# Seven products in place of eight for twelve block pairs of a float32 projection, and weight staging moved one stage later

## The chip, the cores and the metric

One NeuronCore of one Trainium2 chip runs the kernel. The metric is the device time of one execution in microseconds (us). Five engines work side by side, each through its own instructions in order: TensorE (PE), VectorE (DVE), ScalarE (ACT), GpSimd (POOL), and SyncE (SP), whose one queue issues all the DMAs that matter here.

## What is computed

The kernel is one inference step of a two-layer decoder trunk over 1032 token columns: 1024 of a prompt and 8 of single-token samples. The part that the change touches is the end of layer 0, cut from the reference:

```
q, k, v, g, a_low, hb, gate_b, gate_c, z_b = split(h @ w_in)   # h = rmsnorm(x), 1024 wide
o = gla(q, k, v, ...) ; o = rmsnorm(o) * silu(g)
y = causal_dwconv(gate_c * hb, buf, w_sconv)                   # 3 taps, "short convolution"
y = gate_b * y * silu(z_b)
x = x + concatenate([o, y]) @ w_out                            # output projection, 2048 -> 1024
```

Layer 1 follows: a pointwise projection of 1024 to 3072 with a gate, a depthwise convolution 31 wide, a LayerNorm, a second gate, a projection of 1024 to 1024, and a final norm.

## The kernel before, in words

**Products.** Activations lie with channels on partitions and tokens along the free axis. The 1032 columns are cut into three chunks `CH` of 384, 384 and 264. A weight block is 1024 x 128, stored as 128 x 1024 (eight slices of 128 x 128, one for each k). Weights and activations are each split into a rounded high part and the rest, and a product is the sum of three passes in the order `"hxw"`: high by high, high weight by low activation, low weight by high activation. So one block and one chunk make a `unit` (L232) of 8 x 3 = 24 matmuls into one PSUM bank, and a block costs three units.

**Weights.** `plan` lists the blocks in the order of use. `load_ahead` issues the load into one of two `raw` buffers (L199). `split_ahead` lets ACT write the high part `wh` (L219) and POOL the rest `wl` (L220), into pools of three buffers each. `W(key, ahead)` hands out a block and splits `ahead` blocks further. Layer 1's 32 blocks are split earlier by `stage_weights` (L182 to L190): load `pw`, ACT `ph` (L186), POOL `pl` (L187), two stores of 0.5 MB to DRAM (`wh_d`, `wl_d`), so that layer 1 only loads the two parts.

**Order.** ACT's instructions run as the program is written. The tile scheduler orders the other engines by its own estimates. Side work (staging, the state of the long convolution) is a generator that `tick()` moves on after each unit, once a count has been reached: `start(job, at)`. A ring of 25 tiles (`T`) serves nearly all the intermediate tiles, and four PSUM banks the units.

**Short convolution** (L620 to L658). For each of eight i it takes four blocks: gate_c into `cs` (L626), hb into `ch` (L630), three taps on ACT and DVE (L633 to L640), z_b into `zs` with silu (L647, L649), then POOL multiplies `y` by the norm `rs` (L650) and by `zs` (L651), and the gate_b units end it (L655), with the high and low part of `y` written chunk by chunk into `Bm` (L656, L657). Staging starts in it at tick 20 (`STAGE_AT`), and `conv_state` at tick 52.

**Output projection** (L663 to L720). The o tiles are read back from DRAM (`ol`), ACT and DVE write their high and low parts into `O` (L669, L670; `O` takes the buffers of the normed input `A`). Each of eight f runs three units of 48 matmuls, the eight `Bm` terms and the eight `O` terms together:

```
        wy = W("o", f, 1)
        wo = W("o", f, 0, ahead=1)
        for c, (lo, n) in enumerate(CH):
            terms = [(wy[0][:, k * P:(k + 1) * P], ..., Bm[k][1][:, s]) for k in range(KT)] + a_terms(wo, O, c)
```

## Time and profile before

| | |
|---|---|
| median of 3 runs | 1323.96 us (1322.83 to 1327.75) |
| the profiled execution, its own time | 1324.79 us |
| its span, first to last instruction | 1323.0 us |
| GLA with its projections | 0 to about 381 us of the span |
| short convolution | about 381 to 741 us |
| output projection | 741 to about 923 us |
| layer 1 and the final norm | 923 to 1323 us |
| PE, DVE, POOL, ACT busy | 97%, 54%, 49%, 37% |
| DMA | 171.55 MB, mean 130 GB/s |

The stage bounds are read from the lines that the engines run. The profiled execution lies 0.83 us above the median, and 1.79 us of its time lie outside the span. A window's columns are its length, then busy time and instruction count of each engine, the granted TensorE clock as a share of full speed, the mean busy share of the 16 DMA engines, and the rate.

### The profile page before, as it was taken

To read this page: it belongs to the slowest core of one execution; us is meant where nothing else is said; L and a number is where in the kernel's file an instruction comes from. 1 tells how busy PE (TensorE), PEld (TensorE's weight loads), DVE (VectorE), ACT (ScalarE), POOL (GpSimd) and SP (SyncE) were. 2 spreads that over 40 slices of the span, in tenths; PEclk is the share of its full clock that TensorE was granted. 3 is DMA by queue.
4 is the path that set the end of the run, shared out by engine and by line. 5 is a ranking of instruction groups with operands and counts; after the bars stand their busy time and mean duration, and the time that the engine had idled before them with its cause. 6 is when DMAs were issued, how large, how long until landed. Compare 5 with 4: busy or idle time off the path is not lost.

```text
span 1323.0 us, 20294 instructions
## 1 busy us (share of the span) xinstructions
PE 1286.8 (97%) x8333; PEld 1263.3 (95%) x8333; DVE 711.5 (54%) x1081; ACT 492.4 (37%) x753; POOL 651.4 (49%) x400
## 2 busy tenths in 40 slices
PE   7999999998999999999999999999999999999995
PEld 7999999997999999999999999999899999998995
DVE  6444547648546223434424411114769899979726
ACT  7422515233323132222322411113373737437513
POOL 1354525426254357667675221212288898947202
PEclk9999999999999999999999999999899999999997
DMA  7013033221231176777674731213222223223413
GB/s 254 33 64 132 32 97 118 96 96 68 93 138 70 59 255 241 256 267 264 245 271 164 258 117 49 85 45 111 72 94 90 88 91 100 96 96 117 172 64 128
DMA packets 59068, 171.55 MB, mean 130 GB/s; under 512 B 7248, under 2 KB 21296, under 8 KB 58976
## 3 DMA queue, kind: packets, MB, share of 16 engines
q1 hardware_dynamic: 58704, 169.99, 36.6%
q8 instruction: 65, 1.06, 0.3%
q10 hardware_dynamic: 272, 0.27, 0.1%
q14 instruction: 27, 0.22, 0.1%
HBM read 118.06 MB, written 52.18 MB: 129 GB/s over the span
## 4 chain that ended last, share of the span: by engine, by line
PE 79%; DVE 7%; DMA 7%; POOL 2%; ACT 2%; issue 1%; SPq 0%; DVEq 0%; POOLq 0%; ACTq 0%
PE mm L238 66%; PE mm L314 8%; DMA pw<-in_dram 6%; DVE s L541 1%; ACT ph L186 1%; PE g L532 1%; DVE cv L904 1%; DVE x L684 1%; PE g L475 1%; PE g L535 1%; PE g L514 1%; PE g L476 1%; POOL wl L220 1%; DMA s<-in_dram 1%; DVE Y L998 1%
## 5 line engine op out<-in xcount | busy, mean ns | idle before, releaser
L238 PE MATMUL mm<-A,wh 128*128 128x384 f32 (+1 forms) x2304 | 388.1, 319 | 1.4 <-DVE zs L647 1.4
L238 PEld LDWEIGHTS mm<-A,wh 128*128 128x128 f32 x2304 | 364.9, 188 | 2.9 <-DVE zs L647 2.0
L220 POOL TENSOR_TENSOR wl<-wr,wh 128x1024 fp32r<-128x1024 f32 x70 | 176.1, 2519 | 242.3 <-ACT wh L219 125.3
L238 PE MATMUL mm<-A,wl 128*128 128x384 f32 (+1 forms) x1152 | 204.0, 318 | 0.0
L238 PE MATMUL mm<-X,wh 128*128 128x384 f32 (+1 forms) x1152 | 199.3, 323 | 3.4 <-ACT X L686 2.4
L238 PEld LDWEIGHTS mm<-X,wh 128*128 128x128 f32 x1152 | 184.2, 189 | 8.3 <-ACT X L686 5.1
L238 PEld LDWEIGHTS mm<-A,wl 128*128 128x128 f32 x1152 | 184.7, 188 | 0.0
L187 POOL TENSOR_TENSOR pl<-pw,ph 128x1024 fp32r<-128x1024 f32 x32 | 78.8, 2463 | 78.0 <-ACT ph L186 64.7
L785 POOL TENSOR_TENSOR pa<-pa,pr 128x1024 f32<-128x1024 f32 x45 | 110.6, 2458 | 13.0 <-ACT pr L783 10.8
L314 PE MATMUL mm<-wh,A 128*128 128x256 f32 (+3 forms) x576 | 108.8, 288 | 6.9 <-ACT A L259 6.9
L219 ACT ACTIVATE wh<-wr 128x1024 fp32r<-128x1024 f32 (+1 forms) x72 | 75.3, 1052 | 82.1 <-PE mm L238 65.3
L238 PE MATMUL mm<-X,wl 128*128 128x384 f32 (+1 forms) x576 | 103.9, 321 | 0.0
L771 DVE SCALAR_TENSOR_TENSOR g<-u,late,g 128x512 f32<-128x512 f32 x150 | 102.2, 748 | 1.3 <-ACT g L768 1.3
L314 PEld LDWEIGHTS mm<-wh,A 128*128 128x128 f32 (+1 forms) x576 | 87.5, 182 | 8.8 <-ACT A L259 6.9
L238 PEld LDWEIGHTS mm<-X,wl 128*128 128x128 f32 x576 | 94.0, 191 | 0.1
L314 PE MATMUL mm<-wl,A 128*128 128x256 f32 (+3 forms) x288 | 82.8, 288 | 0.0
L704 DVE TENSOR_TENSOR x<-mm,x 128x384 f32<-128x384 f32 (+1 forms) x24 | 12.4, 515 | 126.0 <-PE mm L238 126.0
L186 ACT ACTIVATE ph<-pw 128x1024 fp32r<-128x1024 f32 x32 | 33.9, 1058 | 118.9 <-DMA pw<-in_dram 114.3
L238 PE MATMUL mm<-M,wh 128*128 128x384 f32 (+1 forms) x384 | 66.5, 324 | 2.8 <-ACT M L920 1.7
L238 PE MATMUL mm<-O,wh 128*128 128x384 f32 (+1 forms) x384 | 68.2, 319 | 0.0
L238 PEld LDWEIGHTS mm<-M,wh 128*128 128x128 f32 x384 | 61.9, 191 | 4.2 <-ACT M L920 2.0
L238 PEld LDWEIGHTS mm<-O,wh 128*128 128x128 f32 x384 | 61.5, 188 | 0.1
(225 smaller groups left out, 1906.5 us busy)
## 6 DMA issues: line engine op xcount, KB each, us to landing
wr<-in_dram SPq DMA_DIRECT2D x70, 512.0 KB, 3.6
pw<-in_dram SPq DMA_DIRECT2D x32, 512.0 KB, 5.5
wh_d<-ph SPq DMA_DIRECT2D x32, 512.0 KB, 3.8
wl_d<-pl SPq DMA_DIRECT2D x32, 512.0 KB, 4.5
wh<-wh_d SPq DMA_DIRECT2D x32, 512.0 KB, 3.5
wl<-wl_d SPq DMA_DIRECT2D x32, 512.0 KB, 4.4
bc<-dec_d SPq DMA_DIRECT2D x12, 512.0 KB, 5.7
o_d<-o SPq DMA_DIRECT2D x8, 516.0 KB, 2.9
```

Of the source, the lines that this page charges most:

```text
L186: act.activation(h, r, AF.Copy)
L187: pool.tensor_tensor(out=l, in0=r, in1=h.bitcast(F32), op=ALU.subtract)
L219: act.activation(h[:, :n], raw[:, :n], AF.Copy)
L220: e.tensor_tensor(out=l[:, :n], in0=raw[:, :n], in1=h[:, :n].bitcast(F32), op=ALU.subtract)
L238: pe.matmul(out, wl if p == "w" else wh, xl if p == "x" else xh, start=(i == 0), stop=(i == len(seq) - 1))
L314: pe.matmul(ps[:m, :width], x, y[:, ks], start=(i == 0), stop=(i == 23))
L475: pe.matmul(ps[:, j * P:(j + 1) * P], ke[:, lo:lo + P], qe[:, lo:lo + P], start=True, stop=True)
L476: pe.matmul(ps[0:64, j * P + 64:(j + 1) * P], kd[:, lo:lo + 64], qe[:, lo + 64:lo + P], start=True, stop=True)
L514: pe.matmul(ps[:, j * DV:(j + 1) * DV], kt[:, p_, :], V[Q][:, p_ % 4, :], start=True, stop=True)
L532: pe.matmul(ps[:, j * P:(j + 1) * P], V[Q][:, j, hs], scT[:, Q, j * P:(j + 1) * P], start=True, stop=(p_ == 0))
L771: dve.scalar_tensor_tensor(out=acc[r], in0=u[:, 1 - r, lo + j:hi + j], scalar=df(r, j), in1=acc[r], op0=ALU.mult, op1=ALU.add)
L785: pool.tensor_tensor(out=ac, in0=ac, in1=pr, op=ALU.add)
```

## The change

**Seven products.** The 32 blocks of the short convolution are taken in 16 pairs q (gate_c with hb, then gate_b with z_b). For q = 3 to 14 the first two chunks of a pair, which are 2 blocks x 2 halves of k x 2 chunks = 8 products of 12 matmuls, are done by Strassen's scheme in Winograd's form (`pair_products`): seven `product`s of 12 matmuls, with sums and differences of weights (`pair_sums`, four DVE additions of 128 x 512, whose results `s0` and `s1` are split like a block) and of activations (`build_t`, from tick 10, into twelve tiles `tq` that stay in the ring). The third chunk keeps its unit. ACT copies the first product to `u2`, DVE adds up the others, and `done` multiplies the 768 columns by the norm afterwards. `first_pair` overwrites half of `A[1]` with one of the differences, and `put_back` restores it before q = 15. The first three pairs and the last one run units as before.

**Gated y.** z_b and gate_b now come in one pair, so `y` is finished by POOL (times `gt`, times `zs`) at the end of each i, stored to DRAM (`y_d`), and for i < 7 read back at the end (`all_parts`) to be split into `Bm`. The last one is split from `y` itself after `finish()`, ahead of `O` in the program.

**Output projection.** Each f except the last first runs the three `O` units of 24 matmuls, then the three `Bm` units into the same banks (`into=sums[c]`).

**Staging.** `conv_state` and `stage_weights` start in the output projection, and only 11 blocks go through the latter. Sixteen go through the weight pool as entries `("stage", n)` between the o blocks, with two stores each. The last five of the final projection are not staged: they are loaded and split where they are used.

```diff
-OSQ_WAIT, STATE_AT = 4, 52
+OSQ_WAIT, STATE_AT = 4, 1
...
-STAGE_AT = 20
+STAGE_AT, BUILD_AT = 4, 10
+STRASSEN = range(3, 15)
+RING_STAGED, OWN_STAGED = 11, 16
...
+    for q in range(2 * KT):
+        m0, m1 = blocks_of(q)
+        if q in STRASSEN:
+            for part, src in (("w0", flat(wa[m0])), ("s0", flat(wa[m1])), ("s1", None), ("w1", None)):
+                plan.append(((part, q), src, KT * P, pool, wp))
+        else:
+            plan_a(m0)
+            plan_a(m1)
...
+    owned = list(range(RING_STAGED, RING_STAGED + OWN_STAGED))
     for f in range(KT):
-        for j in (1, 0):
+        for j in (0, 1):
             plan_w(("o", f, j), woa[f, j], pool)
-
-    staged = []
-
-    def plan_d(key, src):
-        plan.append((key, len(staged), KT * P, None, None))
-        staged.append(src)
-
-    for i in range(KT):
-        for j in (8, 0):
-            plan_d(("c", j + i), wic[j + i])
-    for i in range(KT):
-        plan_d(("c", 16 + i), wic[16 + i])
-    for f in range(KT):
-        plan_d(("f", f), woc[f])
-    raws, parts, used = [], [], [0]
+            if owned:
+                plan.append((("stage", owned[0]), flat(staged[owned.pop(0)]), KT * P, pool, wp))
...
+    for i, key in enumerate(keys):
+        if i < RING_STAGED + OWN_STAGED:
+            plan.append((key, i, KT * P, None, None))
+        else:
+            plan_w(key, staged[i], pool)
...
-        for i, src in enumerate(staged):
+        for i, src in enumerate(staged[:RING_STAGED]):
...
+            key, src, n, e, where = plan[len(parts)]
             raw = raws[len(parts)]
+            if key[0] == "s0":
+                pair_sums(key[1])
+            if key[0] in ("s0", "s1"):
+                raw = sums_of[key[1]][key[0] == "s1"]
+            elif key[0] == "w1":
+                raw = raws[len(parts) - 2]
...
+            if key[0] == "stage":
+                sp.dma_start(out=wh_d[key[1]], in_=h[:, :n].bitcast(F32))
+                sp.dma_start(out=wl_d[key[1]], in_=l[:, :n].bitcast(F32))
+
+    def pair_sums(q):
+        if q not in sums_of:
+            e0 = next(i for i, p in enumerate(plan) if p[0] == ("w0", q))
+            load_ahead(e0 + 2)
+            a, b = raws[e0], raws[e0 + 1]
+            s0, s1 = T([P, KT * P], s="s0"), T([P, KT * P], s="s1")
+            lo, hi = slice(0, 512), slice(512, 1024)
+            dve.tensor_tensor(out=s0[:, lo], in0=b[:, lo], in1=b[:, hi], op=ALU.add)
+            dve.tensor_tensor(out=s0[:, hi], in0=s0[:, lo], in1=a[:, lo], op=ALU.subtract)
+            dve.tensor_tensor(out=s1[:, lo], in0=a[:, lo], in1=b[:, lo], op=ALU.subtract)
+            dve.tensor_tensor(out=s1[:, hi], in0=a[:, hi], in1=s0[:, hi], op=ALU.subtract)
+            sums_of[q] = s0, s1
...
+    def unit(c, terms, mid=None, into=None, part=(True, True)):
+        out = mm_t()[:, :CH[c][1]] if into is None else into
         seq = [(t, p) for p in ORDER for t in terms] if ORDER[0] != "k" else [(t, p) for t in terms for p in ORDER[1:]]
         for i, ((wh, wl, xh, xl), p) in enumerate(seq):
-            pe.matmul(out, wl if p == "w" else wh, xl if p == "x" else xh, start=(i == 0), stop=(i == len(seq) - 1))
+            pe.matmul(out, wl if p == "w" else wh, xl if p == "x" else xh, start=(into is None and i == 0),
+                      stop=(part[1] and i == len(seq) - 1))
...
-    start(conv_state(), STATE_AT)
-    start(stage_weights(), STAGE_AT)
...
+        for k in range(4):
+            a, b = T([P, 2 * n], s="xa"), T([P, 2 * n], s="xb")
+            for t, kk in ((a, k), (b, k + 4)):
+                sp.dma_start(out=t, in_=xT[:, kk, 0:2 * n])
+                act.activation(t, t, AF.Copy, scale=pcol("g0", kk))
+            ts = [T([P, 2, n], F32R, s="tq") for _ in range(3)]
+            tf = T([P, 2 * n], s="tf")
+            f = [tf[:, :n], tf[:, n:], b[:, :n]]
+            yield
...
+            dve.tensor_tensor(out=f[1], in0=b[:, n:], in1=a[:, n:], op=ALU.subtract)
+            dve.tensor_tensor(out=a[:, n:], in0=a[:, n:], in1=a[:, :n], op=ALU.subtract)
+            dve.tensor_tensor(out=f[0], in0=b[:, n:], in1=a[:, n:], op=ALU.subtract)
+            dve.tensor_tensor(out=f[2], in0=b[:, :n], in1=f[0], op=ALU.subtract)
+            for j in range(3):
+                act.activation(ts[j][:, 0, :], f[j], AF.Copy)
+                pool.tensor_tensor(out=ts[j][:, 1, :], in0=f[j], in1=ts[j][:, 0, :].bitcast(F32), op=ALU.subtract)
...
+    def first_pair():
+        while any(job[0] is built for job in jobs):
+            tick()
+        for k in range(4):
+            act.activation(A[1][:, k, :], T1[k], AF.Copy)
+            dve.tensor_tensor(out=A[1][:, KT + k, :], in0=T1[k], in1=A[1][:, k, :].bitcast(F32), op=ALU.subtract)
+
+    def put_back():
+        lo, n = CH[1]
+        for k in range(4):
+            if k % 2 == 0:
+                x = T([P, 2, n], s="xp")
+                sp.dma_start(out=x, in_=xT[:, k:k + 2, lo:lo + n])
+            split_x(1, k, x[:, k % 2], 0, n)
...
+    def product(w, half, xs):
+        h, l = w
+        out = mm_t()[:, :CH[0][1]]
+        for i, (p, k) in enumerate((p, k) for p in ORDER for k in range(4)):
+            ws = slice((half * 4 + k) * P, (half * 4 + k + 1) * P)
+            pe.matmul(out, (l if p == "w" else h)[:, ws], xs[k][p == "x"], start=(i == 0), stop=(i == 11))
+        tick()
+        return out
+
+    def add(out, ps, t):
+        dve.tensor_tensor(out=out, in0=ps, in1=t, op=ALU.add)
+
+    def pair_products(q, take, d0, d1, done):
+
+
+        n = CH[0][1]
+        e0 = used[0]
+        w0 = W("w0", q)
+        s0, s1 = W("s0", q, ahead=1), W("s1", q, ahead=0)
+        if q == STRASSEN[0]:
+            first_pair()
+        u = T([P, 2, n], s="u2")
+        r00, r01 = d0[0][:, d0[1]:d0[1] + n], d0[0][:, d0[1] + n:d0[1] + 2 * n]
+        r10, r11 = d1[0][:, d1[1]:d1[1] + n], d1[0][:, d1[1] + n:d1[1] + 2 * n]
+        tq = lambda j: [(TQ[j, k][:, 0, :], TQ[j, k][:, 1, :]) for k in range(4)]
+        act.activation(u[:, 0], product(w0, 0, x_quarter(0, 0)), AF.Copy)
+        take(0, 2, unit(2, a_terms(w0, A, 2)))
+        add(r00, product(w0, 1, x_quarter(0, 4)), u[:, 0])
+        w1 = W("w1", q, ahead=0)
+        add(u[:, 1], product(s0, 1, tq(2)), u[:, 0])
+        p5 = product(s0, 0, x_quarter(1, 0))
+        add(r01, p5, u[:, 1])
+        split_ahead(e0 + 5)
+        add(r10, product(s1, 0, tq(3)), u[:, 1])
+        add(r11, p5, r10)
+        take(1, 2, unit(2, a_terms(w1, A, 2)))
+        add(r10, product(w1, 1, tq(4)), r10)
+        done(1, slice(0, 2 * n))
+        if q + 1 in STRASSEN:
+            pair_sums(q + 1)
+        add(r01, product(s1, 1, x_quarter(1, 4)), r01)
+        done(0, slice(0, 2 * n))
...
+    def gated_parts(k, src=None):
+        if src is None:
+            src = T([P, NT], s="yl")
+            sp.dma_start(out=src, in_=y_d[k])
+        bh = T([P, NT], F32R, s="bh")
+        bl = T([P, NT], F32R, s="bl")
+        act.activation(bh, src, AF.Copy)
+        (pool, dve)[k % 2].tensor_tensor(out=bl, in0=src, in1=bh.bitcast(F32), op=ALU.subtract)
+        Bm.append((bh, bl))
+
+    def all_parts():
+        for k in range(KT - 1):
+            gated_parts(k)
+            yield
...
+        def done_ch(m, s):
+            if m == 0:
+                dve.tensor_tensor(out=cs[:, s], in0=cs[:, s], in1=rs2[:, s], op=ALU.mult)
+                d = ch[:, s.start + 2:s.stop + 2]
+                dve.tensor_tensor(out=d, in0=d, in1=cs[:, s], op=ALU.mult)
...
+        if i == KT - 1:
+            put_back()
+            start(all_parts(), 1)
+        (pair_products if q + 1 in STRASSEN else pair_units)(q + 1, take_gz, (gt, 0), (zs, 0), done_gz)
...
-        pool.tensor_tensor(out=y, in0=y, in1=rs, op=ALU.mult)
+        pool.tensor_tensor(out=y, in0=y, in1=gt, op=ALU.mult)
         pool.tensor_tensor(out=y, in0=y, in1=zs, op=ALU.mult)
-        bh = T([P, NT], F32R, s="bh")
-        bl = T([P, NT], F32R, s="bl")
-        for c, s, ps in units(W("a", 24 + i), A):
-            dve.tensor_tensor(out=y[:, s], in0=ps, in1=y[:, s], op=ALU.mult)
-            act.activation(bh[:, s], y[:, s], AF.Copy)
-            dve.tensor_tensor(out=bl[:, s], in0=y[:, s], in1=bh[:, s].bitcast(F32), op=ALU.subtract)
-        Bm.append((bh, bl))
+        if i < KT - 1:
+            sp.dma_start(out=y_d[i], in_=y)
     sp.dma_start(out=scp_o, in_=scp_t)
     sp.dma_start(out=scs_o, in_=scs_t)
     finish()
+    gated_parts(KT - 1, y)
...
+    start(conv_state(), STATE_AT)
+    start(stage_weights(), STAGE_AT)
...
-        wy = W("o", f, 1)
-        wo = W("o", f, 0, ahead=1)
...
+        wo = W("o", f, 0)
+        sums = [None] * 3
+        if not last:
+            for c in range(3):
+                sums[c] = unit(c, a_terms(wo, O, c), part=(True, False))
+                tick()
...
+            if last:
+                ps = unit(c, y_terms(wy, c) + a_terms(wo, O, c), (20, lambda c=c: x1_stat(c - 1)) if c else None)
+            else:
+                ps = unit(c, y_terms(wy, c), into=sums[c])
+                tick()
```

ACT around the first Strassen pair in the changed order (`xa`, `xb` and `tq` are `build_t`'s last tiles, `cs` the taps' first step, `wh_4204` the first weight split of q = 3):

```order
L666 ACTIVATE xa_4145<-xa_4145,prm 128x768
L666 ACTIVATE xb_4146<-xb_4146,prm 128x768
L676 ACTIVATE tq_4151<-tf_4154 128x384
L676 ACTIVATE tq_4152<-tf_4154 128x384
L676 ACTIVATE tq_4153<-xb_4146 128x384
L801 ACTIVATE cs_3972<-ch_3973,prm 128x1024
L805 ACTIVATE cs_3972<-sscs,prm 128x8
L237 ACTIVATE wh_4204<-wr_3863 128x1024
L237 ACTIVATE wh_4214<-s_4208 128x1024
```

The split stands behind the end of `build_t` and behind the taps of the pair before, which need that pair's last unit.

ACT from the last silu to the first `O` parts, before:

```order
L649 ACTIVATE zs_6582<-zs_6582 128x1032
L219 ACTIVATE wh_6674<-wr_6583 128x1024
L656 ACTIVATE bh_6670<-cs_6402 128x384 x2
L656 ACTIVATE bh_6670<-cs_6402 128x264
L669 ACTIVATE O_6764<-ol_6767 128x768
```

and now (`yl` are gated y read back, `cs_6296` the last gated y, which POOL writes after the silu):

```order
L820 ACTIVATE zs_6483<-zs_6483 128x1032
L761 ACTIVATE bh_6709<-yl_6707 128x1032
L761 ACTIVATE bh_6715<-yl_6713 128x1032
L761 ACTIVATE bh_6719<-cs_6296 128x1032
L836 ACTIVATE O_6723<-ol_6726 128x768
```

The silu was four units ahead of `O`; now it follows the last unit of the stage, and three splits of `y` stand between.

SP in the middle of the output projection, before:

```order
L199 DMA wr_7321<-in_dram 128x1024
L719 DMA x_d<-x_7164 128x1032
L199 DMA wr_7332<-in_dram 128x1024
L199 DMA wr_7495<-in_dram 128x1024
L719 DMA x_d<-x_7338 128x1032
```

and now:

```order
L241 DMA wh_d<-wh_7199 128x1024
L201 DMA wl_d<-pl_7154 128x1024
L242 DMA wl_d<-wl_7200 128x1024
L211 DMA wr_7205<-in_dram 128x1024
L211 DMA wr_7305<-in_dram 128x1024
L200 DMA wh_d<-ph_7239 128x1024
L196 DMA pw_7301<-in_dram 128x1024
L201 DMA wl_d<-pl_7240 128x1024
L900 DMA x_d<-x_7195 128x1032
```

SP issued two weight loads and one store for each f; now it issues 19 transfers from one load of x to the next. From the first `pw` (L196) to the last store of a `pl` (L201), which stands just behind the load of f = 5's first block, there are 72 of about 0.5 MB (0.524 MB).

## Rows read from the trace of the kernel before

**Rows 1.** Page: the span and the engines' busy time, share and instructions.

```profile
span 1323.0 us, 20294 instructions
...
PE 1286.8 (97%) x8333; PEld 1263.3 (95%) x8333; DVE 711.5 (54%) x1081; ACT 492.4 (37%) x753; POOL 651.4 (49%) x400
```

**Rows 2.** Page: the chain that ended last, by engine.

```profile
PE 79%; DVE 7%; DMA 7%; POOL 2%; ACT 2%; issue 1%; SPq 0%; DVEq 0%; POOLq 0%; ACTq 0%
```

**Rows 3.** Windows by stage: columns as under the table above.

```profile
550.00:600.00 50.00, 50.00 (x319) 50.00 (x318) 17.80 (x23) 14.20 (x17) 33.46 (x20) 1.00 0.76 266
600.00:650.00 50.00, 49.23 (x320) 48.91 (x319) 19.17 (x25) 13.83 (x16) 37.21 (x22) 1.00 0.73 261
650.00:700.00 50.00, 49.37 (x314) 49.05 (x313) 18.29 (x23) 15.82 (x19) 35.28 (x17) 1.00 0.66 238
...
800.00:850.00 50.00, 50.00 (x323) 50.00 (x322) 7.30 (x14) 7.35 (x11) 9.60 (x4) 1.00 0.18 64
```

**Rows 4.** Timeline, last gate_b block: start, length, instructions in a row, idle before.

```profile
733.87 2.93 PE L238 MATMUL mm<-A,wh 128*128 128x384 f32 x16
...
738.03 2.09 PE L238 MATMUL mm<-A,wh 128*128 128x264 f32 x16
...
740.93 3.95 PE L238 MATMUL mm<-bh,wh 128*128 128x384 f32 x24
```

**Rows 5.** Waits of PE, whole span: total, times, longest.

```profile
PE mm L238 <- DVE zs L647: 1.4, 2, 0.8
```

**Rows 6.** Lines, shapes apart, 385 to 760 us: mean ns, idle before.

```profile
L219 ACT ACTIVATE wh<-wr 128x1024 fp32r<-128x1024 f32 x32 | 33.4, 1046 | 11.1 <-PE mm L238 11.1
...
L220 POOL TENSOR_TENSOR wl<-wr,wh 128x1024 fp32r<-128x1024 f32 x33 | 85.6, 2594 | 32.5 <-ACT wh L219 28.2 <-issue 4.3
...
L186 ACT ACTIVATE ph<-pw 128x1024 fp32r<-128x1024 f32 x32 | 33.9, 1058 | 118.9 <-DMA pw<-in_dram 114.3
...
L633 ACT ACTIVATE cs<-ch,prm 128x1024 f32<-128x1024 f32 x8 | 9.1, 1142 | 34.3 <-DVE ch L630 23.4 <-issue 11.0
...
L656 ACT ACTIVATE bh<-cs 128x384 fp32r<-128x384 f32 x16 | 8.4, 525 | 42.7 <-DVE cs L655 42.7
...
L655 DVE TENSOR_TENSOR cs<-mm,cs 128x384 f32<-128x384 f32 x16 | 8.9, 554 | 40.8 <-POOL cs L651 33.1 <-PE mm L238 7.6
```

**Rows 7.** Timeline, the stage boundary.

```profile
730.41 1.07 ACT L649 ACTIVATE zs<-zs 128x1032 f32<-128x1032 f32 x1 [8.97 <-DVE zs L647]
...
731.62 2.42 POOL L651 TENSOR_TENSOR cs<-cs,zs 128x1032 f32<-128x1032 f32 x1 [3.90 <-ACT zs L649]
...
741.93 8.12 ACT L669 ACTIVATE O<-ol 128x768 fp32r<-128x768 f32 x12
...
742.79 9.51 DVE L670 TENSOR_TENSOR O<-ol,O 128x768 fp32r<-128x768 f32 x12 [0.30 <-ACT O L669]
```

**Rows 8.** Windows, the start of layer 1, and one idle of PE in the GLA.

```profile
922.88:941.98 19.10, 15.70 (x53) 11.79 (x52) 18.93 (x30) 9.07 (x20) 7.88 (x8) 0.73 0.22 84
...
304.00:306.00 2.00, 0.00 (x0) 0.00 (x0) 2.00 (x9) 0.00 (x0) 0.31 (x2) 1.00 0.00 0
306.00:309.00 3.00, 2.71 (x13) 2.71 (x13) 3.00 (x3) 0.00 (x0) 2.98 (x3) 0.51 0.43 175
```

**Rows 9.** Windows with the DMA engines fullest.

```profile
5.00:10.00 5.00, 3.14 (x13) 3.00 (x13) 3.65 (x6) 4.07 (x11) 0.00 (x0) 1.00 1.06 353
570.00:580.00 10.00, 10.00 (x64) 10.00 (x63) 1.55 (x3) 1.67 (x2) 6.11 (x4) 1.00 0.87 300
610.00:620.00 10.00, 10.00 (x66) 10.00 (x66) 1.35 (x3) 2.01 (x2) 3.93 (x4) 1.00 0.91 328
```

**Rows 10.** Timeline, DVE beside POOL in the taps.

```profile
590.34 1.27 DVE L635 SCALAR_TENSOR_TENSOR cs<-ch,prm,cs 128x1024 f32<-128x1024 f32 x1
590.44 3.43 POOL L220 TENSOR_TENSOR wl<-wr,wh 128x1024 fp32r<-128x1024 f32 x1
591.54 2.36 DVE L640 SCALAR_TENSOR_TENSOR cs<-ch,prm,cs 128x8 f32<-128x8 f32 x1
```

69 lines of the change are left out of this document (50 added, 19 removed).

## The prediction

> **What bounds the kernel now.** I read the page first: PE is busy 97% of the span, and the chain that ended last is PE for 79% of it [rows 1, 2]. So work taken off PE counts in full, as long as nothing that PE waits for comes later. The windows then say where. In the short convolution PE is busy without a gap but for two pieces, 0.77 us and 0.63 us [rows 3], which are the 1.4 us that PE waits for DVE's `zs` [rows 5]; DMA runs at 238 to 266 GB/s and POOL is busy 33 to 37 of 50 us there, all of it hidden. In the output projection PE is full as well, and from 800 us on DMA carries only 64 GB/s [rows 3]. The pace of PE is read from starts in the timeline: a unit of 384 columns takes from 733.87 to 738.03, 4.16 us for 24 matmuls, **174 ns each**; one of 264 takes from 738.03 to 740.93, 2.90 us, 121 ns each [rows 4]. A block is 4.17 + 4.17 + 2.90 = 11.25 us, and one f of the output projection, two blocks, 22.5 us.
>
> The measurement can tell about 0.5% from no change, 6.6 us: under 1317.3 us is faster, over 1330.6 us slower.
>
> **The change part by part.** The sum stands against the profiled execution, 1324.8 us.
>
> *Seven products for eight.* Each pair loses 12 matmuls of 384 columns, 12 x 174 ns = 2.09 us; twelve pairs, **-25.1 us**. The Trainium skill (TensorE: Matmul & The Clock Gate, Back-to-back issue gap) gives N/2.4 + 2.5 ns for an isolated matmul, 162.5 ns at 384; by it the saving would be estimated at 23.4 us. The measured pace decides.
>
> *Staging leaves the short convolution.* The 1.4 us of waiting for `zs` fall where DVE stood behind POOL and staging; I take them as gone, **-1.4**.
>
> *The steady pairs.* Added for each are two weight splits (ACT 1.05 us, POOL 2.6 us each), four DVE sums of 128 x 512, seven additions of 384 (0.55 us each) and the norm multiplications of 768 [rows 6]. Against 20.4 us of PE for a pair (84 x 174 ns + 48 x 121 ns), POOL needs four splits, some 10 us, and about 2.5 us more for its share of the multiplications of y; DVE needs some 11 us, ACT 7. All three fit, and splits come 3 to 5 us ahead of use, because `pair_sums` of the next pair stands before the end of this one. What can bite is an eviction behind a DVE sum that waits for POOL: an eight-column DVE operation took 2.36 us beside a POOL split, which itself took 3.43 instead of 2.4 [rows 10]. Four PSUM banks of 2.09 us each cover one such wait, not several. I take **+1**, between 0 and 1.5 us for each pair (18).
>
> *The first pair.* PE cannot start q = 3 before ACT has split its first weight, and that split stands behind the taps of the pair before (L801), which wait for the pair's last eviction, and behind the last step of `build_t`, which DVE begins only after that eviction. From PE's last matmul: 0.6 us to the eviction; three DVE differences of 0.55, which the first ACT copy needs; three such copies of 0.52; the taps' 1.14; the split 1.05 [rows 6]. That is 6.0, and with a small operation behind the taps some 6.5 us. Below it cannot go under 3.5 (eviction, taps, split alone); above, 8, if POOL's parts come late. PE's clock pays too: after PE had stood idle (nothing ran from 304 to 306 us) the next 3 us were granted 0.51 of full speed [rows 8], the 1.2 GHz level, so some 1.3 us of work are lost. **+7.8** (3.5 to 10).
>
> *Putting `A[1]` back* before q = 15 leaves one matmul waiting for an ACT operation behind the taps: **+1** (0.5 to 4). The store and reloading of y, 14 transfers of 0.5 MB in the stage that staging has left, I cost at nothing: that stage gave 266 GB/s to staging [rows 3] and no longer has to. If that cover were gone, the late `yl` would add to the next term.
>
> *The boundary to the output projection.* Before, silu was done four units early (730.41), and PE went straight into the `Bm` terms at 740.93 while ACT wrote the `O` parts in 8.12 us and DVE the rest in 9.51 us [rows 4, 7]. Now silu follows the last unit, and f = 0 begins with `O`. On ACT: eviction 0.6, silu 1.07, two splits of y of 1.05, then the last one, which waits for POOL's product with `zs` (2.42, behind another POOL operation of 2.4). The first `O` part so comes about 6 us after PE's last matmul. DVE has its own low parts of y ahead, 1.3 us each by its nearest row [rows 10] and beside POOL, and starts on `O` at about 10; it needs 9.5 us, so the last low part is there at some 20 us, and the last unit's passes end at 22. The work in it is 11.25 us, three units of `O`; the stall is **+10.7**. Below: DVE starts right behind the first `O` part, at 7, the end is at 18.4, 7.2 us lost. Above: 13, if the later `ol` loads wait for ring tiles. The nearest row agrees: at the start of layer 1, where PE is fed in the same manner, 53 instructions took 19.1 us at a mean granted clock of 0.73; 48 of them are matmuls of two units that take 8.4 us at the pace above [rows 8]. So 10 to 11 us went there, the clock's part included, and I add none for the clock.
>
> *DMA in the output projection.* This is the term I know least. For each f SP issues 19 transfers of 0.524 MB, 10 MB in 22.5 us, 443 GB/s; the fullest windows show 353, 328 and 300 GB/s with the DMA engines 1.06, 0.91 and 0.87 busy [rows 9]. So the ring's staging cannot keep pace with PE, and behind a late `pw` ACT stands (114 us of such waits in the short convolution, hidden there [rows 6]), with the next o block's split in line behind it. The 72 transfers, 37.7 MB, lie between about f = 0.45, when the first is issued, and the start of f = 5, whose first block is loaded just ahead of the last of them: 4.55 x 22.5 = 102 us of PE work, less 1 us for the split. At 353 GB/s they need 107 us: 6 us too long. At 328: 115 us, 14. At 300: 126 us, 25. Below: nothing, if transfers overlap better than any window shows. I take **+6**, by the window with the engines full, since that is the state that a queue always behind would be in. After f = 4.5 only two splits with stores are left, 5 MB per f, 222 GB/s, which the short convolution shows to be bearable; the last five blocks, split where they are used, have a whole block's time each.
>
> Sum: 1324.8 - 25.1 - 1.4 + 1 + 7.8 + 1 + 10.7 + 6 = 1324.8 us against the profiled execution; the median of the runs lies 0.8 lower, so **1324 us**: no change that could be told.
>
> **The rivals.** *DMA is covered and the boundaries are cheap: faster.* With no stall for DMA, 7.2 at the boundary, 5 at the first pair and none in the pairs or at `A[1]`: 1324 - 6 - 3.5 - 2.8 - 2 = **1310 us**. For it: the 72 transfers are loads and stores mixed, and the rate needed, 37.7 MB in 101 us, is 373 GB/s, not far above 353. Against it: no window shows it. The Trainium skill (DMA: Bandwidth & Descriptors, Measured (HBM→SBUF, 128 partitions, SWDGE, issued from GpSimd)) gives 425 GB/s for a single core's 16 MB load; by that rate the estimate is 89 us and no stall, and the time 1318. No run here shows it yet, and the fullest windows speak against.
>
> *DMA becomes the bound of the output projection: slower.* SP's one queue must keep order; a store that waits for a POOL split holds up the weight load behind it. At 300 GB/s, the rate of 570 to 580 us, the stall is 25 us, and the time 1324 + 19 = **1343 us**. It decides from about 335 GB/s downwards, where the stall passes 12.5 us and the time 1330.6. For it: in before's staging stretch the mean was 266 GB/s though nobody hurried. Against it: there nobody hurried.
>
> *The pairs are held up by DVE behind POOL: slower.* At 1.5 us for each pair, 18 us in place of 1: 1324 + 17 = **1341 us**. It decides from 0.7 us per pair. For it [rows 10], and two more splits for POOL in each pair. Against it: staging, which gave POOL half of its load there, is gone, and PE waited 1.4 us in all for DVE. The Trainium skill (SBUF — State Buffer, Who interferes with whom) has it that a DVE instruction with two SBUF inputs contends with a GpSimd instruction that reads SBUF; the row above agrees, and the change's sums and its norm multiplications are of that kind, its additions out of PSUM are not.
>
> **How the numbers follow.** The forecast (1317 to 1331) 0.36; cheap DMA and boundaries 0.34; DMA-bound 0.19; pairs held up 0.11. Faster by over 0.5% takes the first rival and a sliver of the forecast's low end, 0.35; slower both others, 0.30; the rest, 0.35, is within. The range, 1306 to 1342, reaches a few us below the first rival, whose first-pair and boundary terms could be smaller still, and up to the slower cases; one in ten or so lies on each side. The forecast's own range is 1317 to 1331.
>
> **What would show it.** In the changed kernel's profile: the short convolution from its first block to its last should take some 360 - 25 + 9 = 344 us, with one PE idle of 6 to 7 us at the first pair, released by ACT's `wh`, a granted clock near 0.5 after it, and 84 matmuls of 384 per pair at 174 ns. At the boundary PE should wait for ACT's `O` and then for DVE's, 10 to 11 us in all. In the output projection's first half the windows should show 330 to 360 GB/s and PE idle behind ACT's `wh`, in several pieces. The prediction is wrong if those windows show over 370 GB/s and no PE idle, if the pairs show many small waits for DVE, or if the output projection's second half waits for DMA too.

## The result and the profile after

The change is slower: **1358.8 us** (1357.5 to 1359.6, 4 runs) against 1325.9 us, a ratio of 1.0248 with a 95% interval of 1.0221 to 1.0276. 1324 us was forecast, and the range ended at 1342. The page of the changed kernel answers to [rows 1, 2]:

```profile
span 1357.7 us, 20294 instructions
...
PE 1280.9 (94%) x8189; PEld 1251.1 (92%) x8189; DVE 805.3 (59%) x1193; ACT 534.0 (39%) x801; POOL 730.9 (54%) x440
...
PE 74%; DVE 12%; DMA 8%; ACT 3%; POOL 2%; issue 2%; SPq 1%; DVEq 0%; POOLq 0%; ACTq 0%
```

PE has 144 matmuls fewer, as it should, and is busy 6 us less, yet the span grew by 35 us. PE's waits say where it stands still (total, times, longest), to be held against [rows 5]:

```profile
PE mm L273 <- ACT wh L237: 13.5, 6, 3.1
PE mm L273 <- ACT O L836: 11.2, 1, 11.2
...
PE mm L708 <- ACT wh L237: 5.8, 1, 5.8
PE mm L273 <- DVE gt L713: 5.4, 5, 1.1
...
PE mm L273 <- DVE A L296: 2.8, 1, 2.8
...
PE mm L708 <- DVE A L690: 1.6, 1, 1.6
```

The timeline of PE gives the stages: the start of the short convolution, the end of its last `A` matmul, and the first `X` matmul of layer 1. Lengths in us, from the profiled executions:

| | short convolution | output projection | the rest from layer 1 on |
|---|---|---|---|
| before | 363.3 | 181.8 | 400.1 |
| the change | 360.2 | 216.8 | 402.2 |

So the scheme gained 3 us of the 25 in its own stage, and the output projection lost 35. Four places carry it.

*The first pair* (timeline: start, length, what, idle before):

```profile
451.94 1.04 ACT L237 ACTIVATE wh<-wr 128x1024 fp32r<-128x1024 f32 x1
...
453.04 2.93 PE L708 MATMUL mm<-A,wh 128*128 128x384 f32 x8 [5.80 <-ACT wh L237]
...
460.31 3.48 DVE L803 SCALAR_TENSOR_TENSOR cs<-ch,prm,cs 128x1024 f32<-128x1024 f32 x1
...
463.71 2.33 DVE L808 SCALAR_TENSOR_TENSOR cs<-ch,prm,cs 128x8 f32<-128x8 f32 x1
...
466.57 2.09 PE L708 MATMUL mm<-A,wh 128*128 128x384 f32 x4 [1.57 <-DVE A L690]
```

The split comes as forecast. Behind the wait eight matmuls take 2.7 us in place of 1.4, at a granted clock of 0.51 from 453 to 457 us, and a second wait follows, in which DVE stands in the taps: an operation on eight columns takes 2.33 us. From 447.1 to 475.1 us PE does 60 matmuls of 384 and 48 of 264, 16.2 us of work at [rows 4]'s pace: **11.8 us** are lost.

*The pairs and the putting back* show DVE in the same state (timeline):

```profile
716.78 1.15 DVE L296 SCALAR_TENSOR_TENSOR A<-xp,prm,A 128x384 fp32r<-128x384 f32 x2
718.12 5.95 POOL L238 TENSOR_TENSOR wl<-wr,wh 128x1024 fp32r<-128x1024 f32 x2 [8.42 <-ACT wh L237]
...
719.04 2.77 DVE L296 SCALAR_TENSOR_TENSOR A<-xp,prm,A 128x384 fp32r<-128x384 f32 x1
...
721.73 2.35 DVE L808 SCALAR_TENSOR_TENSOR cs<-ch,prm,cs 128x8 f32<-128x8 f32 x1
724.01 2.78 DVE L296 SCALAR_TENSOR_TENSOR A<-xp,prm,A 128x384 fp32r<-128x384 f32 x1
...
726.85 1.97 PE L273 MATMUL mm<-A,wh 128*128 128x384 f32 x5 [2.83 <-DVE A L296]
```

An operation of L296 takes 2.8 us here; two of them had taken 1.15 us together at 716.78, before POOL's splits of 718.12 began. From 710.9 us to the end of the stage's last matmul at 738.7, PE does 96 matmuls of 384 and 48 of 264, 22.5 us of work in 27.8: **5.3 us** are lost. In the pairs between, PE waits 5.4 us for `gt`, in five waits of 1.1 us, which is 0.45 for each of the twelve pairs.

*The boundary* (ACT, POOL, PE and SP):

```profile
730.94 2.40 POOL L238 TENSOR_TENSOR wl<-wr,wh 128x1024 fp32r<-128x1024 f32 x1 [4.56 <-PE mm L273]
...
733.37 0.32 SPq L242 DMA_DIRECT2D wl_d<-wl  x1
...
734.25 2.15 SPq L758 DMA_DIRECT2D yl<-y_d  x4
...
741.28 1.06 ACT L761 ACTIVATE bh<-yl 128x1032 fp32r<-128x1032 f32 x1 [0.23 <-DMA yl<-y_d]
742.25 1.05 ACT L820 ACTIVATE zs<-zs 128x1032 f32<-128x1032 f32 x1
...
744.75 3.35 POOL L822 TENSOR_TENSOR cs<-cs,zs 128x1032 f32<-128x1032 f32 x1
...
748.13 1.06 ACT L761 ACTIVATE bh<-cs 128x1032 fp32r<-128x1032 f32 x1 [2.93 <-POOL cs L822]
749.10 7.41 ACT L836 ACTIVATE O<-ol 128x768 fp32r<-128x768 f32 x10
...
749.98 4.82 PE L273 MATMUL mm<-O,wh 128*128 128x384 f32 x14 [11.24 <-ACT O L836]
```

SP issues the four reloads only behind a store that waits for POOL's split. The silu (L820) waits in ACT's order behind a part of y whose reload, the second of the four, was issued at 734.98 and landed 6.3 us later. The `O` units end at 764.0, 25.4 us after PE's last matmul of the stage for 11.25 us of work: **14.2 us**.

*The output projection* (windows):

```profile
780.00:800.00 20.00, 20.00 (x131) 20.00 (x130) 5.11 (x10) 4.92 (x6) 14.02 (x9) 1.00 1.02 410
820.00:840.00 20.00, 15.57 (x97) 15.15 (x97) 1.96 (x5) 7.23 (x9) 12.67 (x6) 1.00 0.94 338
840.00:860.00 20.00, 19.20 (x124) 18.99 (x123) 2.57 (x5) 5.58 (x7) 10.98 (x5) 1.00 1.02 416
880.00:900.00 20.00, 16.91 (x96) 16.70 (x95) 1.12 (x2) 4.73 (x5) 9.53 (x4) 0.91 0.84 326
```

The transfers run at up to 416 GB/s with the DMA engines full, and PE stands still in between, six times, for 13.5 us in all. With the half clock behind three of the waits, about 21 us of the stage's 35 are lost behind the boundary. The chain that ended last goes through weight loads of 8 to 9 us and POOL's splits by turns:

```profile
807.71 4.75 POOL wl L238 x2
812.48 9.01 DMA wr<-in_dram
...
821.53 4.69 POOL wl L238 x2
826.23 8.17 DMA wr<-in_dram
```

### The profile page after: what moved, and what is told of

The parts are those of the page before. It is cut to its first block, busy times and chain, and to the rows that moved or that the text cites. A ratio compares the mean times of both kernels' runs of the same rounds, so it can differ in the third digit from the quotient of the medians.

```text
span 1357.7 us, 20294 instructions
## 1 busy us (share of the span) xinstructions
PE 1280.9 (94%) x8189; PEld 1251.1 (92%) x8189; DVE 805.3 (59%) x1193; ACT 534.0 (39%) x801; POOL 730.9 (54%) x440
## 4 chain that ended last, share of the span: by engine, by line
PE 74%; DVE 12%; DMA 8%; ACT 3%; POOL 2%; issue 2%; SPq 1%; DVEq 0%; POOLq 0%; ACTq 0%
PE mm L273 51%; PE mm L708 9%; PE mm L350 8%; DMA wr<-in_dram 4%; DMA pw<-in_dram 3%; DVE cs L803 2%; POOL wl L238 1%; DVE cs L808 1%; DVE s L577 1%; PE g L568 1%; PE g L571 1%; PE g L511 1%; DVE cv L1085 1%; DVE cs L806 1%; DVE x L851 1%
## 5 line engine op out<-in xcount | busy, mean ns | idle before, releaser
L238 POOL TENSOR_TENSOR wl<-wr,wh 128x1024 fp32r<-128x1024 f32 x91 | 228.6, 2525 | 201.1 <-ACT wh L237 193.5
L273 PE MATMUL mm<-A,wh 128*128 128x384 f32 (+1 forms) x1536 | 250.3, 314 | 8.6 <-DVE gt L713 5.4
L273 PEld LDWEIGHTS mm<-A,wh 128*128 128x128 f32 x1536 | 233.9, 190 | 11.5 <-issue 6.8
L237 ACT ACTIVATE wh<-wr 128x1024 fp32r<-128x1024 f32 (+1 forms) x93 | 97.1, 1056 | 186.5 <-DMA wr<-in_dram 82.6
L273 PE MATMUL mm<-A,wl 128*128 128x384 f32 (+1 forms) x768 | 130.9, 311 | 0.0
L273 PEld LDWEIGHTS mm<-A,wl 128*128 128x128 f32 x768 | 119.6, 190 | 0.0
L708 PE MATMUL mm<-A,wh 128*128 128x384 f32 x384 | 78.6, 342 | 7.4 <-ACT wh L237 5.8
L273 PE MATMUL mm<-O,wh 128*128 128x384 f32 (+1 forms) x384 | 68.0, 329 | 14.4 <-ACT O L836 11.2
L884 DVE TENSOR_TENSOR x<-mm,x 128x384 f32<-128x384 f32 (+1 forms) x24 | 12.4, 515 | 109.4 <-PE mm L273 95.2
L708 PEld LDWEIGHTS mm<-A,wh 128*128 128x128 f32 x384 | 68.5, 191 | 8.6 <-ACT wh L237 6.0
L238 POOL TENSOR_TENSOR wl<-s,wh 128x1024 fp32r<-128x1024 f32 x24 | 57.8, 2430 | 29.8 <-PE mm L273 29.8
```

Of the source, the lines that this page charges most:

```text
L237: act.activation(h[:, :n], raw[:, :n], AF.Copy)
L238: e.tensor_tensor(out=l[:, :n], in0=raw[:, :n], in1=h[:, :n].bitcast(F32), op=ALU.subtract)
L273: pe.matmul(out, wl if p == "w" else wh, xl if p == "x" else xh, start=(into is None and i == 0), stop=(part[1] and i == len(seq) - 1))
L708: pe.matmul(out, (l if p == "w" else h)[:, ws], xs[k][p == "x"], start=(i == 0), stop=(i == 11))
```

## The experiments

**The scheme alone, and the staging alone.**

```diff
-STRASSEN = range(3, 15)
+STRASSEN = range(0)
```

> The change with its seven-product scheme switched off: all 16 pairs run units, nothing is built or put back, everything else (pairs, y through DRAM, O before Bm, staging in the output projection) stays. Theory A (the losses in the short convolution belong to the scheme, those behind it to the move of the staging): PE works 25 us more, and the first pair's 11.8 us, the 4.9 us at the putting back and the 5.4 us of waits in the pairs go; the boundary's 14 and the output projection's 21 us stay: 1359 + 25 - 22 = 1362 us. Rival (the late reloads of y at the boundary come from the scheme's tiles in the ring): the boundary falls by some 5 us more, 1357 us or less.

1359.2 us, ratio 1.0242 (1.0212 to 1.0272): the same as with the scheme. Its short convolution takes 361.3 us, the change's 360.2. So 144 matmuls bought 1 us there, and the whole loss against before belongs to what was moved (the staging, y's way through DRAM, `O` ahead of `Bm`). The waits of the pairs are gone, the boundary's 11.2 us stay: the rival falls.

**What of the staging.** Three kernels leave parts of it out: all but one block, the own blocks, and the own blocks' stores. Layer 1 then reads blocks of the ring in their place, so its transfers stay.

```diff
-    owned = list(range(RING_STAGED, RING_STAGED + OWN_STAGED))
+    owned = []
...
-        for i, src in enumerate(staged[:RING_STAGED]):
+        for i, src in enumerate(staged[:1]):
...
-            plan.append((key, i, KT * P, None, None))
+            plan.append((key, i % 1, KT * P, None, None))
```

The second kernel has the first and last of these edits, the third kernel the last alone and `pass` for the two stores, both with `% 11` for `% 1`.

> Only the first of layer 1's 27 staged blocks is staged; layer 1 loads that one block's parts in place of all 27, so 26 blocks of weights are left out of its result, while its loads and its matmuls stay in number. Theory A (staging is what PE waits for in the output projection): the 13.5 us of waits for ACT's weight split and the clock's loss behind them go, up to the 2.9 us at the last f, which is a matter of ACT's order: about 1359 - 18 = 1341 us. Rival (the new order of O and Bm units costs it): no change, 1357 to 1360 us.

> The 16 blocks that pass through the weight pool between the o blocks are left out; the 11 through the ring are staged, and layer 1 reads those 11 in turn, so the 16 are left out of its result. Theory A1 (two raw buffers: a weight's load is issued only when POOL has split the block two before, and the own blocks double that chain): the waits go nearly as far as with one block staged, 1341 to 1345 us. Theory A2 (DMA bandwidth): the ring's 33 transfers remain in the first half, 5.5 MB less per f of 10; some of the waits of the first half stay, 1344 to 1350 us.

> The 16 own blocks are loaded and split as before, but their 32 stores are left out, and layer 1 reads the 11 blocks of the ring in turn, so 16 blocks are left out of its result. Theory A1 (the chain of load, split and next load through two raw buffers): the chain stays and each load lands a little sooner; a third of the loss at most goes, 1352 to 1358 us. Theory A2 (bandwidth): a third of the traffic goes, and nearly all of the loss with it, 1341 to 1346 us.

1333.4, 1334.0 and 1339.9 us, below the lowest figure expected by 8, 7 and 1 us. Their output projections take 195.2, 195.0 and 197.8 us. Without the own blocks all the waits for splits there go, the ring's eleven notwithstanding, and without their stores 19 of the 22 us go. That is against the chain through two raw buffers (A1) and for the traffic, or for the stores' place in SP's queue. The next run tells these apart, and the fourth looks at the ring's absence:

```diff
-                sp.dma_start(out=wh_d[key[1]], in_=h[:, :n].bitcast(F32))
-                sp.dma_start(out=wl_d[key[1]], in_=l[:, :n].bitcast(F32))
+                pool.dma_start(out=wh_d[key[1]], in_=h[:, :n].bitcast(F32))
+                pool.dma_start(out=wl_d[key[1]], in_=l[:, :n].bitcast(F32))
```

> The 32 stores of the 16 own blocks are issued by POOL, right behind its split, in place of SP; every transfer stays. Theory Q (a store that waits for ACT's or POOL's split holds up the weight load behind it in SP's one queue): the waits for the o blocks' splits go as far as without the stores, 13 to 19 us less, 1340 to 1346 us, less if POOL pays long for issuing. Theory B (the traffic itself is too much): the same bytes, no gain, 1355 to 1362 us.

```diff
-    start(stage_weights(), STAGE_AT)
...
-            plan.append((key, i, KT * P, None, None))
+            plan.append((key, RING_STAGED + i % OWN_STAGED, KT * P, None, None))
```

> The 11 blocks through the ring are left out, the 16 own blocks stay with their stores; layer 1 reads the 16 in turn, so the 11 are left out of its result. Traffic falls from 10 to 5 MB per f in the first half. Theory B (the sum of the traffic is too much for the DMA engines; either part alone is not): the waits go but for the 2.9 us at the last f, 1336 to 1342 us. Theory A1 (the own blocks' chain through two raw buffers): most of the loss stays, 1348 to 1357 us.

With the stores on POOL's queue: 1354.6 us, and the stage 215.0 of 216.8; PE still waits 13.2 us for splits. SP's order is not it. Without the ring: 1343.6 us, 2 above its range, and of the waits for splits only one is left, the 2.9 us at the last f. The same stretch in four kernels (windows: the change, without the own blocks, without their stores, without the ring):

```profile
764.00:860.00 96.00, 90.77 (x576) 90.14 (x575) 14.91 (x29) 27.46 (x34) 58.38 (x31) 1.00 0.94 353
764.00:860.00 96.00, 96.00 (x615) 96.00 (x614) 17.58 (x32) 26.43 (x33) 51.20 (x27) 1.00 0.81 284
764.00:860.00 96.00, 96.00 (x611) 96.00 (x610) 18.00 (x32) 33.92 (x41) 67.59 (x36) 1.00 0.90 320
764.00:860.00 96.00, 96.00 (x615) 96.00 (x614) 15.52 (x30) 22.94 (x29) 47.91 (x27) 1.00 0.73 265
```

So each staging is free alone but for that one wait, at 13 or 10 transfers for each f, 303 or 233 GB/s asked for, and only the sum, 443, makes PE wait. It is the traffic, not the splits: without the stores ACT and POOL do more of them in this stretch than in the change, and PE is full. Nor do the stores hold up the splits by keeping the weight pool's buffers: in the change, from 764 to 935 us, ACT waits before its splits `wh` for weight loads (54.3 us, 16 times) and never for a store.

**The order of single steps.** y reloaded three ahead and `O` ahead of the silu; `A[1]` put back inside the last pair; the first pair prepared early:

```diff
+        if i == KT - 1:
+            finish()
+            load_o((0, 1))
         tables(SILU)
...
+        if q == STRASSEN[-1]:
+            put_back()
...
-STAGE_AT, BUILD_AT = 4, 10
+STAGE_AT, BUILD_AT = 4, 6
...
+        if q + 1 == STRASSEN[0]:
+            first_pair()
```

> At the end of the short convolution the reloads of y are issued three ahead and two parts are split per unit, and the O parts of the first two chunks are placed ahead of the last silu in ACT's order, the third behind it. Theory (PE's 11.2 us wait for O comes from ACT's order: behind late reloads, silu and the last split of y): PE starts on O within 1 us and the low parts bound it; 8 to 13 us less, 1346 to 1351 us. Rival (the O loads and the tiles of the ring bound it): under 4 us less.

> A[1] is put back in the middle of the last Strassen pair, when its last reader is done, in place of behind the taps. Theory (the DVE half of it waits behind taps that wait for POOL): the 2.8 and 0.35 us of waiting and the clock's loss behind them go, 4 to 5 us less, 1354 us. Rival (DVE is late in any case): under 1.5 us less.

> Building starts at tick 6 in place of 10, the first pair's first weight is split one block ahead, and A[1] is overwritten ahead of the taps. Theory (the first pair's loss is order alone: the split behind the end of the building and the taps): both waits, 5.8 and 1.6 us, go and the clock stays up; 9 to 12 us less, 1347 to 1350 us. Rival (POOL's parts of the building are late and hold the second product): 3 to 6 us less.

1352.8, 1356.3 and 1356.6 us: 6, 2.5 and 2.2 us less, each below what was expected, and the last two, of two runs each, not clear of the noise (ratios 1.0221 and 1.0223, intervals from 1.019 to 1.025). In each, much of the wait that was removed came back in another place. With `O` first, PE starts at once and then waits for DVE's low parts, twelve operations that took 19.0 us in place of 9.5. With the first pair early, ACT's 5.8 us are gone, and

```profile
463.92 1.01 PE L708 MATMUL mm<-tq,wh 128*128 128x384 f32 x2 [5.38 <-DVE gt L789]
```

stands in their place. Putting back early shortened the short convolution by 6 us and lengthened the boundary's wait for ACT's `O` to 14.0. In two of the three DVE was late next, so DVE was changed directly.

**The taps in PSUM.** The same three taps, added up in PSUM banks that lie idle in this stage:

```diff
...
-            dve.scalar_tensor_tensor(out=y[:, :NP], in0=ch[:, j:j + NP], scalar=w3[j], in1=y[:, :NP],
-                                     op0=ALU.mult, op1=ALU.add)
...
+                dve.scalar_tensor_tensor(out=y[:, lo:lo + n] if j == 2 else acc, in0=ch[:, lo + j:lo + j + n],
+                                         scalar=w3[j], in1=acc, op0=ALU.mult, op1=ALU.add)
...
```

> The three taps of the short convolution are added up in PSUM (two banks of 512 columns and one of 8) in place of SBUF, so that DVE's tap instructions have one SBUF input each; everything else as in the change. Theory S (DVE stands behind POOL's splits because of its second SBUF input, and PSUM banks are not emptied meanwhile): the 5.4 us of waits in the pairs go, and of the first pair and the putting back some 2 to 4 us with their clock; 1349 to 1353 us. Rival (DVE simply has too much to do there): no change, 1356 to 1361 us.

**1345.9 us**, 13 less from this alone, more than expected; the short convolution takes 346.1 us. All the waits for `gt` and for `A` L296 are gone. The eight-column operation in the new taps (line numbers of that kernel), beside POOL's splits as before:

```profile
499.88 4.76 POOL L238 TENSOR_TENSOR wl<-s,wh 128x1024 fp32r<-128x1024 f32 x2 [6.15 <-ACT wh L237]
...
501.23 0.22 DVE L810 SCALAR_TENSOR_TENSOR cs<-ch,prm,g 128x8 f32<-128x8 f32 x1
```

0.22 us, where it took 2.35. The operation itself differs by one input less in SBUF. The change's own trace has the other half of the comparison: of its sixteen eight-column operations of two SBUF inputs, fourteen ran beside a POOL operation and took 2.33 to 2.41 us, and two met none and took 0.22, of which one is

```profile
407.73 0.22 DVE L808 SCALAR_TENSOR_TENSOR cs<-ch,prm,cs 128x8 f32<-128x8 f32 x1
```

So it takes both, the second input in SBUF and POOL at work. This is what the Trainium skill (SBUF — State Buffer, Who interferes with whom) states of a DVE instruction with two SBUF inputs and a GpSimd instruction that reads SBUF; the two kernels agree with it.

**All four cures, and where the ring's staging goes.** `cured` has the three edits of order and the taps in PSUM together. The next kernel also moves the ring's staging:

```diff
+    start(stage_weights(), 0)
...
     start(conv_state(), STATE_AT)
-    start(stage_weights(), STAGE_AT)
```

> Taps in PSUM, the first pair prepared early, A[1] put back early, y reloaded three ahead and O ahead of the last silu, all at once; staging as in the change. Theory (DVE behind POOL takes the place of each wait that order alone removes, so the parts add up to more together): 8 for the pairs, 8 to 11 at the first pair, 4 at the putting back, 6 at the boundary, about 1332 us. Rival (each removed wait is replaced by another): the sum of the single runs, 1340 us or more.

> As the run with all four cures, and the 11 blocks through the ring are staged from the short convolution's first unit on, so that only the 16 own blocks are staged in the output projection. Theory B: the output projection then carries 5 MB per f and its waits go, 15 to 20 us less than the run before: 1312 to 1318 us, faster than both kernels. Theory A1: the own blocks' chain stays, 1328 us or more. If POOL's eleven splits in the short convolution hold DVE again, some 5 us come back.

The cures: 1330.3 us, ratio 1.0035 (1.0022 to 1.0048), and a short convolution of **337.3 us**, 24 less than without the scheme. The parts add up to 28.6 us, their single runs to 24; as ratios to the kernel before, measured beside each, it is 2.1% against 2.0%, so that they help each other isn't clear of the noise. The output projection still waits 14.0 us for splits. With the ring's staging in front of and beside the first pair, 1337.2 us: the output projection's waits are down to 2.9 us, as theory B had it, but PE now waits 6.2 us for DVE and 9.1 us for splits around the first pair, and the short convolution is back at 361.5. Work moved again, and a wait with it. So the ring was started inside the pairs, at a wider pace, then the block that the last f waits for was split a unit earlier, and that with the scheme off:

```diff
+        if i == 2:
+            start(stage_weights(), 0)
         q = 2 * i
...
-            yield 0
+            yield 4
```

```diff
+            if f == KT - 2 and c == 1:
+                split_ahead(used[0] + 4)
             if last:
```

> As the run with all four cures, but the 11 blocks through the ring are staged in the steady Strassen pairs, from q = 4 on at about six units a block, so that they meet neither the first pair nor the 16 own blocks. Theory B (the output projection's loss is the sum of both stagings, either alone being free): the waits for ACT's split fall to the 2.9 us of the last f, some 16 us less than with the cures alone, 1311 to 1317 us. Rival (POOL's and DMA's extra work in the pairs holds PE there, as at the first pair): 1322 us or more.

> The run before, with the last f's Bm block split one unit earlier in ACT's order, ahead of the squares of f = 6's last chunk. Theory (the 2.9 us at the last f are ACT's order alone): 3 to 5 us less with the clock's loss, 1307 to 1313 us. Rival (a weight pool of three buffers holds ACT instead): no gain or a loss of some us.

> The run before with the scheme switched off: 16 pairs of units, nothing built or put back, the same placing of the staging, taps in PSUM, y three ahead, O first. Theory (with its waits cured the scheme is worth nearly its 144 matmuls of 174 ns): 22 to 25 us more than the run before, 1330 to 1336 us. Rival (the scheme still pays elsewhere): under 18 us more.

Spread over the steady pairs: 1326.5 us, a miss of 9 to 15; PE waits 8.7 us in the pairs for ACT's splits, so the rival's reading held there; which engine makes them late no run separates. With the last f's block split a unit earlier, 1322.1 us (ratio 0.9961, 0.9949 to 0.9974), 4.5 less as expected. The same with the scheme off, 1330.2 us: the scheme is worth 8 us beside this staging, not 22. Last, the ring in two parts: its first blocks early, the others in the output projection two steps apart. The first kernel has four early blocks of eleven; the other two have rings of 9 and 8 blocks, with two early and one (`stage_weights` now takes the first block, the end, the steps from load to split, and those to the next block):

```diff
+    start(stage_weights(0, 4, 1, 1), 0)
...
-    start(stage_weights(), STAGE_AT)
+    start(stage_weights(4, RING_STAGED, 0, 2), STAGE_AT)
```

> As the best run so far (all cures, the last f's split one unit early), but of the 11 blocks through the ring 4 are staged in the first three pairs, before any Strassen pair, with a longer lead between load and split, and 7 in the output projection at a third of the pace, 14 to 15 transfers per f, some 340 GB/s; none in the Strassen pairs. Theory (the three waits of 2 to 3 us that are left in the pairs come from the ring's staging among DVE's sums and ACT's order, and the output projection bears up to some 400 GB/s): the pairs run without a wait, 10 to 13 us less, 1309 to 1313 us. Rival (340 GB/s is already too much, or the fourth block meets the first pair): 1318 us or more.

> As the run before, with nine blocks through the ring in place of 11: two in the first three pairs and seven in the output projection; the final projection splits seven blocks directly in place of five. Theory (the third and fourth early block met the building and the first pair, and cost the 9 us of waits and half clock that showed there): these go, 1310 to 1314 us, unless the two more direct blocks meet POOL's and DVE's work at the start of the final projection, which gives up to 4 us back. Rival (the building itself, set earlier, is what costs there): no gain, 1320 to 1324 us.

> The same with one early block, seven in the output projection, and all eight blocks of the final projection split directly. Theory: as the run before at the first pair, within 2 us of it; if the eighth direct block comes before POOL is free at the final projection's start, 2 to 5 us slower than it. Rival as there.

Four blocks early and seven in the output projection: 1322.3 us, a miss of 9 to 13, in the rival's range. The pairs behind the first and the output projection behind its boundary run without a wait of note, at up to 380 GB/s, but the first pair loses the gain. With two and with one of the early blocks, 1316.4, 2 above its range, and **1314.2 us**, ratio 0.9893 (0.9876 to 0.9910), 1.1% faster than the kernel before. The last one's windows:

```profile
440.00:460.00 20.00, 19.92 (x129) 19.59 (x128) 16.55 (x25) 9.86 (x16) 13.59 (x10) 1.00 0.14 54
460.00:480.00 20.00, 20.00 (x131) 20.00 (x130) 8.91 (x15) 5.46 (x6) 13.30 (x8) 1.00 0.16 53
...
780.00:800.00 20.00, 20.00 (x128) 20.00 (x127) 3.00 (x6) 6.42 (x8) 11.88 (x6) 1.00 1.00 366
```

Full through the first pair, and full in the output projection with the DMA engines at 1.00. So the early blocks cost the 9 us, not the building. What it lacks to a full 25 us is in its stages: 337.6, 189.4 and 407.4 us, against 363.3, 181.8 and 400.1 before. The output projection keeps some 7 us, 6 of them at its boundary; the rest from layer 1 on is 5 us longer than the change's, where it splits eight blocks directly.

## Why the prediction was wrong

The saving itself was right: once the waits are gone the short convolution is 24.0 us shorter with the scheme than without (337.3 against 361.3), for the 25.1 of the sum. Four terms failed.

*The scheme's own waits, +9.8 in the sum* (1 for the pairs, 7.8 for the first pair, 1 for the putting back): they measured some 22, namely 5.4, 11.8 and 5.3. [Rows 10] had the cause, and the third rival had named it. In the pairs its price wasn't reached (0.45 us per pair, under its 0.7). But the same DVE behind POOL also stood at the first pair, where 1.6 us of waiting followed the 5.8 that the text had as 6.5, and at the putting back, with 2.8; both the text had costed by ACT's order, with DVE at its own pace. Matmuls at half speed came behind these waits, some 4 us of them at the first pair, where 1.3 were taken, and 2 at the putting back. That staging would leave POOL free was taken as evidence against the rival; POOL's two more splits in each pair were enough.

*The boundary, +10.7*: 14.2. The mechanism was right. The step that failed is "the store and reloading of y ... I cost at nothing": the cover named was bandwidth, which was there, but the reload is issued by SP behind loads and stores that wait for POOL, and ACT's silu stands behind it. By the timeline the 3.5 us are these; the run that moved the reloads moved `O` as well, so it doesn't price them alone.

*DMA, +6*: 10.5. Here the size alone was off. From the first load of the ring to the landing of its last store SP issued 72 transfers, as counted, in 109.4 us at a mean of 352 GB/s, where the text has 107 us at 353:

```profile
767.40:876.80 109.40, 101.86 (x636) 101.03 (x635) 16.51 (x33) 33.58 (x42) 67.24 (x33) 0.98 0.95 352
```

PE did 97.9 us of work meanwhile, where the text has 101: the first load came 0.2 f later. That the mean met 353 is in part luck, since [rows 9] aren't the fullest of their trace. The change has windows of 410 and 416 GB/s, and the kernel before had

```profile
757.00:762.00 5.00, 5.00 (x39) 5.00 (x38) 0.56 (x1) 1.58 (x2) 0.00 (x0) 1.00 1.02 417
```

At 416 the text's working gives no stall. Each o block has its own date, two raw buffers give it a lead of one block, and at a rate asked for of 443 GB/s a load takes up to 10 us (6.3 in the median from 764 to 900 us) in place of 3.6. Why 338 GB/s, not 416, was moved just where PE stood still isn't settled: the loads that PE waits for also hold up the next transfers, and no run separates cause and effect there. The second rival's bandwidth limit, deciding at 335 GB/s, isn't what the windows show, though its sign and much of its size came true.

*Behind the ring, 0*: some 10. The step that failed is "After f = 4.5 only two splits with stores are left ... which the short convolution shows to be bearable". f = 5 lost 5.0 us: its wait at 890.2 (3.1 us) is for a load that SP issued at 879.15, in a burst right behind the ring, and that took 9.9 us. The last f's wait of 2.9 us, with the half clock behind it, cost about as much again. That one is ACT's order: it stays without the ring, and the run that splits this block a unit earlier gains 4.5 us. The five direct blocks, also at nothing, held, but for 2 us in the rest.

The clock's part, left out of both, is some 6 us. Behind three of the six waits (at 862.8, 890.2 and 928.8 us) 11 to 18 matmuls take 320 ns each, at a granted clock of 0.50 to 0.53, the 1.2 GHz level; behind the other three it is 1.00. The lengths don't tell them apart: the wait that ended at 836.5 took 2.33 us, the one at 862.8 took 2.31 (windows right behind the two):

```profile
836.60:840.00 3.40, 3.40 (x20) 3.40 (x21) 0.00 (x0) 0.00 (x0) 3.40 (x3) 1.00 0.93 284
863.00:866.60 3.60, 3.60 (x13) 3.60 (x13) 0.00 (x0) 0.00 (x0) 3.60 (x2) 0.53 0.97 280
```

Two of the text's own signs of being wrong came true: waits for DVE in the pairs, and a wait for DMA in the output projection's second half.

## What to carry to other kernels

When PE is full, a scheme that saves matmuls is paid for by the engines that feed it: before costing it, count the instructions with two SBUF inputs on DVE that it or the work beside it puts next to POOL, since each may wait for POOL's (2.3 to 2.4 us for an operation of 0.22 here); accumulating in an idle PSUM bank took that away for 13 us here. Work that is hidden by a stage isn't free in the next one: put it where its transfers and those already there ask for less than the windows were seen to move (303 GB/s asked for cost nothing here, 443 some 15 us, a third of it behind the traffic's end), and check each load that PE waits for against its own date. A wait that was removed by order alone mostly showed what was late next, so judge such cures together as well as one by one.

## What was not expected of the hardware

The DMA engines moved 410 to 416 GB/s over 20 us, mixed loads and stores, where the fullest 20 us of the kernel before (609 to 629) held 313, and its fullest 5 us 417. That is near the 425 GB/s which the Trainium skill (DMA: Bandwidth & Descriptors, Measured (HBM→SBUF, 128 partitions, SWDGE, issued from GpSimd)) gives for one large load. And an operation on eight columns cost DVE 2.35 us beside POOL, ten times its 0.22, by the place of one input.
